# The squares of three group norms: transposed and summed by VectorE, instead of multiplied by a column of ones

## The chip, the cores and the metric

One core of a Trainium2 chip runs the whole program. The time is the device time of one execution in microseconds (us); lower is better. The kernel before takes 617.97 us, the median of three runs (617.78 to 618.43).

Engines, by the names that the profile uses: PE is TensorE's matmul, PEld its weight load, DVE is VectorE, ACT is ScalarE, POOL is GpSimd, SP is SyncE, which issues the DMAs.

## The reference

A two-layer encoder over 256 positions of width 1024, in fp32. Each layer has a mixer of three kinds of attention heads (4 neighbourhood heads "a", 6 dilated heads "d", 6 grouped-query heads "c", each 64 wide) and a channel sublayer (gate, up, a convolution of three taps, gelu, down). What the change touches is the norm of each group's output before the output projection:

```python
def rms_norm(x, g):
    xf = x.astype(jnp.float32)
    y = xf * lax.rsqrt(jnp.mean(xf * xf, axis=-1, keepdims=True) + EPS)
    return (y * g.astype(jnp.float32)).astype(x.dtype)
...
    mix = jnp.concatenate([
        rms_norm(out_a, og[:NA_W]),
        rms_norm(out_d, og[NA_W:NA_W + DIL_W]),
        rms_norm(out_c, og[NA_W + DIL_W:]),
    ], axis=-1)
    return x + mix @ w_out_l
```

So each of the three groups needs, for every one of the 256 positions, the sum of squares over its 256 or 384 columns.

## The kernel before

**Arithmetic.** Large products keep fp32 accuracy by splitting each operand into a high part and a rest (`_hi`/`_lo`, or `act_ch`/`act_cl` for the attention weights): three products stand for one. Weights come by DMA (`wp_raw`); ScalarE casts the high part (`wp_hi`), VectorE subtracts it for the rest (`wp_lo`).

**Layout.** The outputs of the heads stand transposed: 128 features on the partitions, the 256 positions along the free axis, two heads to a tile. When the second head of a pair has been weighed, `mixed` (L1032) makes four things of the pair's PSUM tile: ScalarE writes the high part times the gain (`act_mixT_hi`), VectorE the rest (`act_mixT_lo`), ScalarE the squares (`act_sqm`), and GpSimd adds the squares of the group's pairs up. `group_rstd` (L1047) then has one 128x256 tile of squares and needs the sum over its partitions, with positions on partitions at the end. It is two fp32 products, one for each half of the 256 positions: the squares are the stationary operand, a 128x1 column of ones moves, and each gives one column of a PSUM tile. VectorE copies the two columns out (`small_ss`), and two GpSimd instructions make the factor (`small_ms`, then `small_rstd`). The profile shows each fp32 product as two MATMULs with two weight loads.

**Stages of a layer.** (1) The input projections, as filler between the preparation of queries and keys. (2) Sixteen heads in the order d, c, a: `scores` for a pair of heads (L1126), the softmax (`softens`, L977: maxima on VectorE, two exps and two normalising multiplications for each head on ScalarE, in `act_s2k` tiles), `turn` (L1007: four transposes, then ScalarE's cast `act_ch` and VectorE's rest `act_cl`), `weigh` (L1023: products of `act_ch` and `act_cl` with the values). A `Weave` (L665) puts products of the output projection of the groups that are complete (`out_projections`, L826, tiles `psa_a`) between the heads' work. `group_rstd` is called after the weighing of head 7 (group d), of head 12 (group c) and, for group a, once all heads and the filler are done (L1209). (3) The entrance to the channel sublayer (L1211 to L1267). The last output projections run, first for the left 512 columns, then for the right ones. Each closes with a VectorE instruction that adds the PSUM tile times `small_rstd` to the residual (`const_x`). PE transposes `const_x` in eight 128x128 blocks for each half, ScalarE makes the high part of `act_hT` from them, VectorE the rest. The first block of the gate-and-up products has 16 products with the left half, then needs the right half's transposes. (4) Gate, up and down products, which keep PE busy to the end of the layer.

That makes three group sums a layer and six in all, 12 fp32 products.

**What sets the order.** Nothing is issued as it is written. A `Plan` records every operation, simulates a list schedule with a price for each operation (`cost`, L414), a fixed handover time between engines and a rank that `later(...)` shifts, and emits every engine's stream in the order that this gives. All rows of the profile therefore carry the line of that one emitting statement, L411. The prices that matter here:

```python
        if method == "transpose":
            return 110, 0
        n = args[2].width()
        if args[1].dtype == F32:
            return 108, 0
...
        if method in ("reduce_sum", "reduce_max"):
            n = args[1].width()
```

A VectorE copy or reduction from PSUM is priced at 1.04 ns a column plus 70. Changing one operation's price moves everything that is planned behind it, on all engines.

Of the kernel before, what the change touches and what calls it, by code (L numbers as in the profile page):

```python
# [11 lines left out]
F32 = mybir.dt.float32  # L12
# [4 lines left out]
AX = mybir.AxisListType  # L17

P = 128
S = 256  # L20
NT = S // P
# [198 lines left out]
class Plan:  # L220
# [5 lines left out]
    def pool(self, real, name, bufs, space=bass.MemoryType.SB):  # L226
        return PlanPool(self, real, name, bufs, space)
# [226 lines left out]
def encoder_kernel(  # L454
# [21 lines left out]
    nc = Plan(tc)  # L476
# [3 lines left out]
    const = pool("const", 1)  # L480
# [13 lines left out]
    ident = const.tile([P, P], F32, tag="ident", name="ident")  # L494
# [33 lines left out]
    minus_half = const.tile([P, 32], F32, tag="mh", name="minus_half")  # L528
    nc.gpsimd.memset(minus_half, -0.5)

    ones = const.tile([P, 1], F32, tag="ones", name="ones")
    nc.gpsimd.memset(ones, 1.0)

    vown, vkv = (
        [const.tile([P, NT, 2 * n + 1, HD], F32R, tag=f"v{n}{i}", name=f"v{n}{i}") for i in range(2)]
# [79 lines left out]
    def rstd_of(ss, n, width, eps, name):  # L615

        ms = small.tile([P, n], F32, tag="ms", name=f"ms_{name}")
        nc.gpsimd.tensor_scalar(ms, ss, 1.0 / width, eps, ALU.mult, ALU.add)
        r = small.tile([P, n], F32, tag="rstd", name=f"rstd_{name}")
        nc.gpsimd.tensor_tensor(r, ms, minus_half[:, :n], op=ALU.pow)  # L620
        return r
# [168 lines left out]
    for l in range(DEPTH):  # L790
# [256 lines left out]
        def group_rstd(gi):  # L1047

            _, n = OUTP[gi]
            ps = psw.tile([P, 512], F32, tag="w", name=f"gs{gi}{l}")  # L1050
            for t in range(NT):
                nc.tensor.matmul(
                    ps[:, t : t + 1], hold["sq", gi][:, t * P : (t + 1) * P], ones, start=True, stop=True
                )
            ss = small.tile([P, NT], F32, tag="ss2", name=f"ss_m{gi}{l}")
            nc.vector.tensor_copy(ss, ps[:, :NT])
            group_r[gi] = rstd_of(ss, NT, n * P, EPS, f"m{gi}{l}")
            wv.give(f"mix{gi}")


        hold, turned = {}, {}
# [133 lines left out]
        for i in range(len(heads) + 2):  # L1195
            for part in range(3):
                if (i, part) in hooks:
                    with nc.later(PREP_LATER):
                        hooks[i, part]()
                if part == 0 and i < len(heads) and i % 2 == 0:  # L1200
                    scores(i)
                elif part == 1 and 0 <= i - 1 < len(heads):
                    heads[i - 1].turn()
                elif part == 2 and 0 <= i - 2 < len(heads):
                    weigh(i - 2)
                    if i - 2 in (7, 12):
                        group_rstd((i - 2) // 12)
        wv.fill(1e9)
        group_rstd(2)  # L1209


# [207 lines left out]
```

## Time and profile before

| | us |
|---|---|
| median of three runs (range) | 617.97 (617.78 to 618.43) |
| the profiled execution, device time | 617.81 |
| its span in the profile | 616.0 |
| PE busy | 606.0 |
| DVE busy | 485.8 |
| ACT busy | 428.8 |
| POOL busy | 77.4 |

The device time of the profiled execution is 1.8 us longer than its span; that stretch lies around what the profile covers. The granted clock of TensorE was 0.999 of full speed over the run.

How its rows are read: a row of a timeline has a start, a time in us, the engine, the line, the operation, its output and inputs by the program's names, the tile shapes, and how many neighbouring instructions it groups. A bracket holds the idle time before it and what released it. A matmul's row includes the time until its result is out, so neighbouring rows overlap, and the pace of PE is read from one start to the next.

### The profile page before, as it was taken

What the parts mean: (1) busy time and instruction counts of PE and PEld (TensorE: products, weight loads), DVE (VectorE), ACT (ScalarE), POOL (GpSimd) and SP (SyncE); (2) the same over time, 40 slices, a digit from 0 to 9 for tenths busy, and PEclk for the clock granted to TensorE, in tenths of its full rate; (3) what the DMA queues carried; (4) which work ended last, traced back from release to release, by engine and by line L of the source; (5) the groups of instructions that cost most, each with busy time, mean ns of one, the idle gap of its engine ahead of it and who ended that gap; (6) DMA issues with size and microseconds to landing.
All of it is one profiled execution on the core that took longest, in us unless ns stands there. A gap on an engine that the chain in (4) does not pass through costs nothing.

```text
span 616.0 us, 9844 instructions
## 1 busy us (share of the span) xinstructions
PE 606.0 (98%) x3496; PEld 524.8 (85%) x3496; DVE 485.8 (79%) x1000; ACT 428.8 (70%) x1064; POOL 77.4 (13%) x125
## 2 busy tenths in 40 slices
PE   8999999999999999999999999999999999999997
PEld 6999878888888888888899989887888888888886
DVE  4898988897877877777867798979877777777775
ACT  6888989686566565556588899897756565566551
POOL 2731230211500000000023212112000000000000
PEclk9999999999999999999999999999999999999999
DMA  8894311755596555655444632127575555555501
GB/s 284 274 291 146 103 38 37 245 195 197 183 231 222 178 197 204 199 169 162 155 148 150 233 104 86 34 73 243 182 238 173 191 205 186 169 192 204 168 40 68
DMA packets 81617, 104.66 MB, mean 170 GB/s; under 512 B 9480, under 2 KB 69224, under 8 KB 81568
## 3 DMA queue, kind: packets, MB, share of 16 engines
q1 hardware_dynamic: 81024, 103.78, 52.0%
q8 instruction: 27, 0.44, 0.3%
q10 hardware_dynamic: 544, 0.26, 0.1%
q14 instruction: 22, 0.18, 0.1%
HBM read 102.54 MB, written 1.49 MB: 169 GB/s over the span
## 4 chain that ended last, share of the span: by engine, by line
PE 93%; ACT 3%; DVE 2%; DMA 1%; issue 1%; SPq 0%; ACTq 0%; DVEq 0%
PE psw_w L411 49%; PE psa_a L411 44%; ACT act_s2k L411 2%; DMA wp_raw<-in_w_in_dram 1%; DVE act_hT L411 1%; DVE wp_lo L411 1%; DVE const_x L411 0%; ACT wp_hi L411 0%; ACT act_hT L411 0%; ACT act_ch L411 0%; SPq L411 0%; DVE act_cl L411 0%; DVE act_z L411 0%; ACT const_v L411 0%; DVE small_nm L411 0%
## 5 line engine op out<-in xcount | busy, mean ns | idle before, releaser
L411 DVE TENSOR_TENSOR wp_lo<-wp_raw,wp_hi 128x512 fp32r<-128x512 f32 (+2 forms) x348 | 243.9, 729 | 49.7 <-ACT wp_hi L411 47.8
L411 PE MATMUL psw_w<-act_hT,wp_hi 128*128 128x512 f32 x704 | 247.6, 397 | 2.0 <-DVE act_hT L411 2.0
L411 ACT CAST wp_hi<-wp_raw 128x512 fp32r<-128x512 f32 (+2 forms) x348 | 212.7, 660 | 29.3 <-PE psw_w L411 15.6
L411 PE MATMUL psw_w<-act_hT,wp_lo 128*128 128x256 f32 x704 | 195.7, 279 | 0.0
L411 PEld LDWEIGHTS psw_w<-act_hT,wp_hi 128*128 128x128 f32 x704 | 131.8, 188 | 34.1 <-DVE act_hT L411 3.2
L411 PEld LDWEIGHTS psw_w<-act_hT,wp_lo 128*128 128x128 f32 x704 | 132.6, 188 | 1.2
L411 PE MATMUL psa_a<-wp_hi,act_hT 128*128 128x384 f32 (+2 forms) x448 | 113.1, 333 | 1.3 <-ACT act_hT L411 1.2
L411 ACT COPY act_s2k<-psw_w 128x256 f32<-128x256 f32 x88 | 32.3, 372 | 80.2 <-PE psw_w L411 80.2
L411 PEld LDWEIGHTS psa_a<-wp_hi,act_hT 128*128 128x128 f32 x448 | 77.9, 189 | 4.5 <-ACT act_hT L411 1.6
L411 PE MATMUL psa_a<-wp_lo,act_hT 128*128 128x384 f32 (+2 forms) x224 | 74.6, 334 | 0.0
L411 PE MATMUL psa_a<-wp_lo,act_ch 128*128 128x512 f32 x176 | 69.5, 395 | 0.0
L411 PE MATMUL psa_a<-wp_hi,act_ch 128*128 128x512 f32 x176 | 69.3, 394 | 0.0
L411 PE MATMUL psa_a<-wp_hi,act_cl 128*128 128x512 f32 x176 | 66.1, 394 | 0.0
L411 DVE TENSOR_TENSOR act_s2k<-psw_w,act_s2k 128x256 f32<-128x256 f32 x88 | 36.8, 422 | 32.4 <-ACT act_s2k L411 31.9
L411 PEld LDWEIGHTS psa_a<-wp_lo,act_hT 128*128 128x128 f32 x224 | 42.2, 189 | 1.9 <-DVE wp_lo L411 1.0
L411 PEld LDWEIGHTS psa_a<-wp_hi,act_cl 128*128 128x128 f32 x176 | 33.2, 188 | 7.7
L411 PEld LDWEIGHTS psa_a<-wp_hi,act_ch 128*128 128x128 f32 x176 | 33.1, 188 | 7.8
L411 PEld LDWEIGHTS psa_a<-wp_lo,act_ch 128*128 128x128 f32 x176 | 33.1, 188 | 6.9
L411 DVE SCALAR_TENSOR_TENSOR act_s2k<-act_s2k,act_cw,act_s2k 128x255 f32<-128x255 f32 x88 | 36.7, 476 | 1.4 <-ACT act_s2k L411 1.3
L411 POOL TENSOR_TENSOR small_rstd<-small_ms,const_mh 128x6 f32<-128x6 f32 (+2 forms) x26 | 32.0, 1232 | 2.2
L411 ACT ACTIVATE act_s2k<-act_s2k,act_cw 128x256 f32<-128x256 f32 x44 | 24.1, 595 | 11.6 <-DVE act_s2k L411 11.6
L411 PE MATMUL psw_w<-act_ch,const_v 128*128 128x256 f32 x128 | 28.5, 287 | 1.6 <-ACT act_s2k L411 1.1
(109 smaller groups left out, 754.3 us busy)
## 6 DMA issues: line engine op xcount, KB each, us to landing
wp_raw<-in_w_gate_up_dram SPq DMA_DIRECT2D x44, 1024.0 KB, 5.0
wp_raw<-in_w_down_dram SPq DMA_DIRECT2D x22, 1024.0 KB, 4.8
wp_raw<-in_w_in_dram SPq DMA_DIRECT2D x14, 768.0 KB, 5.9
wp_raw<-in_w_in_dram SPq DMA_DIRECT2D x8, 1024.0 KB, 5.9
wp_raw<-in_w_out_dram SPq DMA_DIRECT2D x8, 768.0 KB, 4.3
wp_raw<-in_w_out_dram SPq DMA_DIRECT2D x4, 512.0 KB, 3.8
act_nab<-dram_scr SPq DMA_DIRECT2D x4, 448.0 KB, 7.0
out_dram<-const_x SPq DMA_DIRECT2D x4, 256.0 KB, 2.0
```

The costliest lines, as they stand in the source:

```text
L411: getattr(o.engine.real, o.method)(*map(real, o.args), **{k: real(v) for k, v in o.kw.items()})
```

## The change

`ones` and its memset go away. In `group_rstd` the two products with the column of ones become two transposes of the squares' halves, which fill 256 columns of the same PSUM tile. The copy of two columns becomes a VectorE sum over the 128 columns of each half. What comes before (the squares and GpSimd's additions) and after (`small_ms`, `small_rstd`) is as it was.

```diff
-    ones = const.tile([P, 1], F32, tag="ones", name="ones")
-    nc.gpsimd.memset(ones, 1.0)
...
             ps = psw.tile([P, 512], F32, tag="w", name=f"gs{gi}{l}")
             for t in range(NT):
-                nc.tensor.matmul(
-                    ps[:, t : t + 1], hold["sq", gi][:, t * P : (t + 1) * P], ones, start=True, stop=True
-                )
+                cols = slice(t * P, (t + 1) * P)
+                nc.tensor.transpose(ps[:, cols], hold["sq", gi][:, cols], ident)
             ss = small.tile([P, NT], F32, tag="ss2", name=f"ss_m{gi}{l}")
-            nc.vector.tensor_copy(ss, ps[:, :NT])
+            nc.vector.reduce_sum(ss, ps[:, :S].rearrange("p (t d) -> p t d", d=P), axis=AX.X)
             group_r[gi] = rstd_of(ss, NT, n * P, EPS, f"m{gi}{l}")
```

The planner now prices each of the two PE operations at 110 instead of 108, and VectorE's at 1.04 x 256 + 70 = 336 instead of 72. From the first group sum of each layer to the entrance of its channel sublayer it gives another order; outside these two stretches (about 90 to 129 us and 390 to 430 us in the profile) the order stays. On SP one pair of DMAs (the convolution's weights of layer 0) is issued one weight load later.

The names in the rows below have buffer numbers, which differ between the programs because one constant is gone. First, PE in layer 0, where the heads of group a are scored for the second time (`act_ko`, `act_qo`: the scores; `act_s2k`: the attention weights to be transposed; `act_ch`, `act_cl` with `const_v`: the weighing). Before:

```order
L411 MATMUL psa_a_157<-wp_lo_252,act_mixT_hi_911 128x512
L411 MATMUL psw_w_123<-const_ident_92,act_s2k_166 128x128
L411 MATMUL psa_a_157<-wp_hi_243,act_mixT_lo_951 128x512
L411 MATMUL psw_w_123<-const_ident_92,act_s2k_166 128x128 x3
L411 MATMUL psw_w_168<-act_ch_858,const_v_107 128x256
L411 MATMUL psw_w_121<-act_ko_567,act_qo_443 128x256
```

Now:

```order
L411 MATMUL psa_a_336<-wp_hi_135,act_mixT_lo_949 128x512
L411 MATMUL psw_w_121<-act_ch_750,const_v_105 128x256
L411 MATMUL psw_w_166<-const_ident_90,act_s2k_164 128x128 x4
L411 MATMUL psw_w_121<-act_cl_768,const_v_105 128x256
L411 MATMUL psw_w_121<-act_ch_750,const_v_110 128x256
L411 MATMUL psw_w_121<-act_ch_750,const_v_105 128x256
L411 MATMUL psw_w_121<-act_cl_768,const_v_105 128x256
L411 MATMUL psw_w_121<-act_ch_750,const_v_110 128x256
L411 MATMUL psw_w_121<-act_ch_856,const_v_105 128x256
```

The first product with the second cast (`act_ch_858` before, `act_ch_856` now) stood right behind the transposes, with the scores behind it; five products of the other head now stand between, and the scores follow after the whole weighing.

Second, ACT in layer 1, at the second sum (group c). `act_s2k` with `small_nm` is an exp, with `small_rs` a normalising multiplication; `act_sqm` are the squares that the second sum waits for; `act_ch` is the cast that the weighing waits for. Before:

```order
L411 ACTIVATE act_mixT_hi_911<-psw_w_168,const_gains_127 128x256
L411 ACTIVATE act_sqm_1006<-psw_w_168 128x256
L411 CAST wp_hi_137<-wp_raw_155 128x512
L411 ACTIVATE act_s2k_177,small_rs_815<-act_s2k_166,small_nm_806 128x256 x2
L411 ACTIVATE act_s2k_131,small_rs_830<-act_s2k_81,small_nm_817 128x256
L411 ACTIVATE act_s2k_177<-act_s2k_177,small_rs_815 128x256 x2
L411 ACTIVATE act_s2k_131,small_rs_830<-act_s2k_81,small_nm_817 128x256
L411 CAST act_ch_858<-psw_w_89 128x512
L411 ACTIVATE act_s2k_131<-act_s2k_131,small_rs_830 128x256 x2
L411 CAST act_ch_752<-psw_w_123 128x512
```

Now:

```order
L411 CAST act_ch_856<-psw_w_87 128x512
L411 ACTIVATE act_mixT_hi_909<-psw_w_121,const_gains_125 128x256
L411 ACTIVATE act_s2k_175,small_rs_813<-act_s2k_164,small_nm_804 128x256 x2
L411 ACTIVATE act_s2k_129,small_rs_828<-act_s2k_81,small_nm_815 128x256 x2
L411 ACTIVATE act_s2k_175<-act_s2k_175,small_rs_813 128x256 x2
L411 ACTIVATE act_s2k_129<-act_s2k_129,small_rs_828 128x256 x2
L411 ACTIVATE act_sqm_1004<-psw_w_121 128x256
L411 CAST act_ch_750<-psw_w_119 128x512
L411 CAST wp_hi_135<-wp_raw_153 128x512 x2
```

The squares stood ahead of all four exps and now stand behind four exps and four multiplications; the cast stood ahead of the last two multiplications and now stands behind all of them and the squares.

Third, PE in layer 1 at the entrance to the channel sublayer. `psa_a` rows are the last output projections, `const_x` rows the transposes of the residual, `act_hT` the first gate-and-up product. Before:

```order
L411 MATMUL psa_a_304<-wp_lo_146,act_mixT_hi_911 128x512
L411 MATMUL psw_w_121<-const_ident_92,const_x_79 128x128
L411 MATMUL psw_w_123<-const_ident_92,const_x_79 128x128
L411 MATMUL psa_a_304<-wp_hi_137,act_mixT_lo_951 128x512
L411 MATMUL psa_a_338<-wp_hi_137,act_mixT_hi_911 128x512
L411 MATMUL psw_w_121<-const_ident_92,const_x_79 128x128 x3
L411 MATMUL psw_w_123<-const_ident_92,const_x_79 128x128 x3
L411 MATMUL psa_a_338<-wp_lo_146,act_mixT_hi_911 128x512
```

Now:

```order
L411 MATMUL psa_a_336<-wp_hi_135,act_mixT_hi_909 128x512
L411 MATMUL psa_a_336<-wp_lo_144,act_mixT_hi_909 128x512
L411 MATMUL psa_a_336<-wp_hi_135,act_mixT_lo_949 128x512
L411 MATMUL psw_w_119<-const_ident_90,const_x_79 128x128
L411 MATMUL psw_w_87<-const_ident_90,const_x_79 128x128
L411 MATMUL psw_w_119<-const_ident_90,const_x_79 128x128 x3
L411 MATMUL psw_w_87<-const_ident_90,const_x_79 128x128 x3
L411 MATMUL psw_w_121<-act_hT_142,wp_hi_241 128x512
```

Before, 20 products of the output projection were left behind the third sum, 13 ahead of the transposes, two among them, five behind. Now 15 are left behind the third sum, and all of them stand ahead of the transposes; five have moved ahead of the sum.

## Prediction

> **What bounds the kernel now.** First the busy times, the granted clock and the chain that ended last, from the page:
>
> ```profile
> PE 606.0 (98%) x3496; PEld 524.8 (85%) x3496; DVE 485.8 (79%) x1000; ACT 428.8 (70%) x1064; POOL 77.4 (13%) x125
> PEclk9999999999999999999999999999999999999999
> PE 93%; ACT 3%; DVE 2%; DMA 1%; issue 1%; SPq 0%; ACTq 0%; DVEq 0%
> ```
>
> PE is busy in 98% of the span and 93% of the chain is PE. So two things change the time: what PE has to do, and the few places where PE stands still. DVE and ACT have room on average, and count where PE waits for them. Those places I looked for in PE's timeline, in the stretches that the new order touches. Layer 0, the heads of group a; the 405.45 row is the same work in layer 1:
>
> ```profile
> 101.86 0.38 PE L411 MATMUL psw_w<-act_ch,const_v 128*128 128x256 f32 x1 [0.34 <-ACT act_ch L411]
> 102.18 1.44 PE L411 MATMUL psw_w<-act_ko,act_qo 64*128 64x256 f32 x12
> 103.55 0.39 PE L411 MATMUL psw_w<-act_cl,const_v 128*128 128x256 f32 x1
> 405.45 0.98 PE L411 MATMUL psw_w<-act_ko,act_qo 64*128 64x256 f32 x12
> 406.36 0.55 PE L411 MATMUL psw_w<-const_ident,act_s2k 128*128 128x128 f32 x3
> ```
>
> PE stands still for 0.34 us until ACT's cast is there. The 12 scores then take 1.37 us to the next start (103.55 - 102.18), where undisturbed ones take 0.91 (406.36 - 405.45): 0.46 more. This place costs 0.8 us. The other two are the entrances to the channel sublayers, with the transposes of the residual and the first products of each half:
>
> ```profile
> 124.11 0.50 PE L411 MATMUL psw_w<-act_hT,wp_hi 128*128 128x512 f32 x1
> 128.74 0.50 PE L411 MATMUL psw_w<-act_hT,wp_hi 128*128 128x512 f32 x1 [0.69 <-DVE act_hT L411]
> ```
>
> ```profile
> 423.84 0.47 PE L411 MATMUL psa_a<-wp_lo,act_mixT_hi 128*128 128x512 f32 x1
> 424.15 0.39 PE L411 MATMUL psa_a<-wp_hi,act_mixT_lo 128*128 128x512 f32 x1
> 424.38 0.40 PE L411 MATMUL psa_a<-wp_hi,act_mixT_hi 128*128 128x512 f32 x1
> 425.20 0.50 PE L411 MATMUL psw_w<-act_hT,wp_hi 128*128 128x512 f32 x1
> 428.11 1.03 PE L411 MATMUL psw_w<-const_ident,const_x 128*128 128x128 f32 x8
> 430.48 0.50 PE L411 MATMUL psw_w<-act_hT,wp_hi 128*128 128x512 f32 x1 [1.34 <-DVE act_hT L411]
> ```
>
> Behind 128.74 and 430.48 PE is kept busy to the end of the layer. I therefore measure the change by how much earlier or later these two products start; what is gained or lost there reaches the end.
>
> **The change part by part. PE's own work.** A pair of products with ones, and transposes of the same kind of tile:
>
> ```profile
> 89.17 0.60 PE L411 MATMUL psw_w<-const_ident,act_s2k 128*128 128x128 f32 x4
> 89.60 0.50 PE L411 MATMUL psw_w<-const_ones,act_sqm 128*128 128x1 f32 x4
> 89.97 0.48 PE L411 MATMUL psa_a<-wp_lo,act_mixT_hi 128*128 128x512 f32 x1
> 121.14 0.38 PE L411 MATMUL psw_w<-const_ident,const_x 128*128 128x128 f32 x2
> 121.27 0.48 PE L411 MATMUL psa_a<-wp_hi,act_mixT_hi 128*128 128x512 f32 x1
> ```
>
> From start to start a pair of products (four rows) takes 89.97 - 89.60 = 0.37 us. Four transposes take 89.60 - 89.17 = 0.43, so two take 0.21; the two of `const_x` take 0.13. I take 0.21, since its input is the same kind of fp32 tile as the squares. The saving is 0.16 a pair (0.24 by the other row), 0.5 us a layer, 1.0 in all.
>
> **VectorE's sum.**
>
> ```profile
> L411 DVE COPY small_ss<-psw_w 128x2 f32<-128x2 f32 x6 | 0.9, 155 | 0.5 <-PE psw_w L411 0.3
> L411 DVE TENSOR_REDUCE small_nm<-psw_w 128x1 f32<-128x256 f32 x24 | 8.7, 416 | 2.5 <-PE psw_w L411 1.8 <-ACT act_s2k L411 0.6
> L411 DVE TENSOR_REDUCE small_ss<-act_s2k 128x8 f32<-128x512 f32 x4 | 2.6, 678 | 0.8 <-ACT act_s2k L411 0.8
> L411 DVE COPY act_rb<-psw_w 128x256 f32<-128x256 f32 x2 | 0.8, 424 | 0.6 <-PE psw_w L411 0.6
> ```
>
> A reduction of 256 columns from PSUM takes 416 ns, the copy 155. One with eight results over 512 columns takes 678, half of it 339. So the sum costs between 0.18 and 0.26 us more than the copy; I take 0.26, from the row with the same columns. [...]
>
> In the groups d and c the sum is behind the heads' work: the products that need its `small_rstd` only close with it, several us later, and DVE is idle 21% of the time. I price these four at nothing; without that cover they would cost 4 x 0.26 = 1.0. The third sum is different: nothing is left to do but the last output projections, which need it.
>
> ```profile
> 419.41 0.27 PE L411 MATMUL psw_w<-const_ident,act_s2k 88*128 88x88 f32 x1
> 420.11 1.03 POOL L411 TENSOR_TENSOR small_rstd<-small_ms,const_mh 128x2 f32<-128x2 f32 x1
> 421.17 1.41 DVE L411 SCALAR_TENSOR_TENSOR const_x<-psa_a,small_rstd,const_x 128x512 f32<-128x512 f32 x2
> ```
>
> The row with 88 columns follows directly behind the third sum on PE and serves as its mark. `small_rstd` is ready 1.73 us after it (421.14 - 419.41), with the new sum 1.99. The two additions to `const_x` take 1.41 more.
>
> **The new order in layer 0.** The scores that stood between two late casts now follow behind the whole weighing, and five more products stand ahead of the second cast's first user. At 0.12 us each (half the 0.23 that 512 columns take at 424.15) these cover 0.6 us, more than the 0.34 of idle time, and the scores no longer stand behind a half-served pair of PSUM tiles. I take the whole 0.8 as saved. With the three pairs (0.5) the third sum's mark comes 1.3 earlier, and less 0.26 for VectorE the first `act_hT` product 1.04 earlier, at 123.07.
>
> Then a loss. Before, seven of the right half's transposes stood among the left half's 16 products; now all eight stand behind them. Sixteen products take 428.11 - 425.20 = 2.91 us in layer 1, where nothing stands among them, and eight transposes 8 x 0.107 = 0.86. From the last transpose to the first product that uses it there are two rows to go by: 1.36 (423.84 to 425.20), and 0.85 from the last one of layer 0:
>
> ```profile
> 126.07 0.93 PE L411 MATMUL psw_w<-const_ident,const_x 128*128 128x128 f32 x7
> 126.75 0.36 PE L411 MATMUL psw_w<-act_hT,wp_lo 128*128 128x256 f32 x1
> ...
> 127.78 0.27 PE L411 MATMUL psw_w<-const_ident,const_x 128*128 128x128 f32 x1
> ```
>
> (127.78 + 0.11 to 128.74.) I take 1.1. So 123.07 + 2.91 + 0.86 + 1.1 = 127.94 against 128.74: layer 0 **gains 0.8**.
>
> **The new order in layer 1.** Here ACT becomes late for the second sum and for the cast that the weighing waits for:
>
> ```profile
> 406.12 0.36 ACT L411 ACTIVATE act_sqm<-psw_w 128x256 f32<-128x256 f32 x1
> 406.93 0.51 ACT L411 ACTIVATE act_s2k<-act_s2k,small_nm 128x256 f32<-128x256 f32 x1
> 408.09 0.51 ACT L411 ACTIVATE act_s2k<-act_s2k,small_nm 128x256 f32<-128x256 f32 x1
> 408.60 0.90 ACT L411 ACTIVATE act_s2k<-act_s2k,small_rs 128x256 f32<-128x256 f32 x2
> 409.40 0.49 ACT L411 ACTIVATE act_s2k<-act_s2k,small_nm 128x256 f32<-128x256 f32 x1
> 409.89 0.56 ACT L411 CAST act_ch<-psw_w 128x512 fp32r<-128x512 f32 x1
> 410.51 0.38 PE L411 MATMUL psw_w<-act_ch,const_v 128*128 128x256 f32 x1 [0.15 <-ACT act_ch L411]
> ```
>
> The first exp starts when its maxima are there, 406.93. Four of them at 0.5 (408.9, or 409.1 if the third starts no earlier than the 408.09 of before), four multiplications at 0.42 (410.8), the squares at 0.36 (411.2), the cast at 0.5 (411.7). Before, this cast was done at 410.45. PE is ready at about 410.7 and waits about 1.1 us where it waited 0.15: **+0.95**. Queued behind it are the second sum, the transposes of the next heads and the fillers behind them; they all move back by as much.
>
> At the entrance five projection products have moved ahead of the third sum: 5 x 0.23 = 1.15. Its mark comes at 419.41 - 0.5 + 0.95 + 1.15 = 421.0. `small_rstd` is ready at 423.0, `const_x` at 424.4; PE has 15 products left, to 421.0 + 15 x 0.23 = 424.5. So both meet, and the transposes start there. Then 0.86 for the eight of them and 1.36: first `act_hT` product at 426.7, against 425.20. With 2.91, 0.86 and 1.1 the second comes at 431.6, against 430.48: layer 1 **loses 1.1**. It is less than at the first because before DVE was late there by its own queue of casts.
>
> **Sum.** -0.8 + 1.1 = +0.3 on the profiled execution's 617.81, so 618.1. The median of the runs shown is 0.16 above that execution: **618.3 us**, no change that a measurement of this kernel can tell (it tells 0.2%, 1.24 us).
>
> **Rivals.**
> 1. **Faster, 616.4.** ACT's lateness in layer 1 is absorbed: the maxima are ready earlier than 406.93, or PE arrives later (-0.95). The pairs take 0.13 (-0.5), and both tails 0.85 instead of 1.1 (-0.5). For it speaks that PE has fewer cycles to spend in any case; against it that four multiplications and the squares really stand ahead of the cast.
> 2. **Slower, 619.6.** In layer 0 PE waits for ACT's cast at another place: the 0.8 is not saved, since the same exps and multiplications have to come before the same casts. The late transposes cost the longer tail, 1.36, in both layers (+0.5). It ends slower once 0.9 of that 1.3 comes about. For it: every new wait found above is on ACT's casts. Against it: the 5 products really are cover.
> 3. **The transposes save nothing on PE**, 619.3: a pair takes the 0.37 of the products, because something other than the number of products sets the pace of this tile (+1.0). Against it the 0.43 for four transposes.
> 4. **The clock falls, 620.5.** Transposes alone are on PE from 424.5 to 426.7. If the clock were halved for as long as they stand without a product, it would cost 2.2 us. Against it this row (sum, then PE, PEld, DVE, ACT and POOL busy, clock, DMA share):
>
> ```profile
> 425.00:432.00 7.00, 5.66 (x34) 4.69 (x33) 7.00 (x15) 6.14 (x15) 2.15 (x3) 1.00 0.72 263
> ```
>
> From 428.11 to 430.48 only transposes ran, for 2.37 us, at a granted clock of 1.00. [...] This trace shows no effect at this length.
>
> **How the numbers follow.** The forecast 0.42, rival 1 0.22, rival 2 0.30, rival 3 0.04, rival 4 0.02. Faster by over 0.2% is rival 1, slower are rivals 2 to 4 together (0.36). The forecast's own range is 616.8 to 619.2. The whole range goes down to 616.2, where layer 1 loses nothing by ACT and the pairs and tails take their lower rows, and up to 620.3, which holds rivals 2 and 3 and the longer tails and uncovered sums in part on top of them.
>
> **What would show it.** Right: pairs of transposes of `act_sqm` at 0.21 from start to start; `small_ss` reductions near 0.42; at 101 to 104 no idle time before `act_ch` products and scores in 0.9; an idle time of about 1 us before an `act_ch` product near 411; `act_hT` second products near 127.9 and 431.6. Wrong: an idle time at other casts of ACT in either layer (rival 2), no idle time near 411 (rival 1), pairs at 0.37 (rival 3), a granted clock under 1 at the entrances (rival 4), or a new stall where the order was not changed.

## The result and the profile after

| | before | changed |
|---|---|---|
| median of 20 executions, us | 618.19 | 619.05 |
| range | 617.57 to 618.68 | 617.80 to 621.36 |
| ratio, 95% interval | | 1.0020 (1.0014 to 1.0026) |
| the profiled execution, device time (span) | 617.81 (616.0) | 620.22 (618.4) |

Slower by 0.86 us in the median: under the 1.24 us that were called a difference, though the interval lies above 1. The spread has grown, and that is the first thing to look at. In 13 of the 20 executions of the changed kernel the mean granted clock was 0.999 or 1.0, and their median is 618.93. In the other seven it was 0.996 or 0.997, and their median is 620.22. The profile is of such an execution. Its page:

```profile
PE 607.4 (98%) x3484; PEld 525.0 (85%) x3484; DVE 488.6 (79%) x1000; ACT 429.0 (69%) x1064; POOL 78.7 (13%) x124
PEclk9999999999999999999999999998999999999999
PE 91%; ACT 4%; DVE 2%; issue 1%; DMA 1%; POOL 1%; SPq 0%; DVEq 0%; ACTq 0%; POOLq 0%
```

One slice of 40 has an 8 where before had a 9. It is layer 1's entrance to the channel sublayer. The windows of the changed kernel (us; PE, PEld, DVE, ACT and POOL busy, clock, DMA share, GB/s), the third of them the row that the prediction showed of before:

```profile
422.91:426.32 3.41, 1.59 (x11) 1.12 (x10) 3.34 (x7) 3.41 (x10) 0.00 (x0) 1.00 0.63 251
426.32:429.74 3.42, 3.42 (x12) 2.94 (x12) 3.42 (x7) 2.38 (x7) 1.85 (x3) 0.50 0.13 33
425.00:432.00 7.00, 5.52 (x24) 4.63 (x24) 5.06 (x11) 4.80 (x14) 1.85 (x3) 0.76 0.41 137
```

PE's timeline of the changed kernel there:

```profile
418.85 0.38 PE L411 MATMUL psw_w<-const_ident,act_sqm 128*128 128x128 f32 x2
419.07 0.24 PE L411 MATMUL psw_w<-const_ident,act_s2k 88*128 88x88 f32 x1
...
422.45 0.40 PE L411 MATMUL psa_a<-wp_hi,act_mixT_lo 128*128 128x512 f32 x1
422.68 0.40 PE L411 MATMUL psw_w<-const_ident,const_x 128*128 128x128 f32 x2
423.30 0.87 PE L411 MATMUL psw_w<-const_ident,const_x 128*128 128x128 f32 x6 [0.22 <-DVE const_x L411]
425.77 0.53 PE L411 MATMUL psw_w<-act_hT,wp_hi 128*128 128x512 f32 x1 [1.60 <-DVE act_hT L411]
...
430.26 1.04 PE L411 MATMUL psw_w<-const_ident,const_x 128*128 128x128 f32 x8
432.30 0.50 PE L411 MATMUL psw_w<-act_hT,wp_hi 128*128 128x512 f32 x1 [1.01 <-DVE act_hT L411]
```

From the last output projection to the first `act_hT` product there are 3.32 us with eight transposes only (422.45 to 425.77). Half a microsecond after PE is at work again, its clock goes to a half for 3.42 us. The 16 products take 4.49 us (425.77 to 430.26) where they took 2.91: 1.58 lost.

Layer 0 is earlier, as forecast. The same three places of the changed kernel as in the prediction's first fences, the scores, the first and the second `act_hT` product:

```profile
101.39 0.60 PE L411 MATMUL psw_w<-const_ident,act_s2k 128*128 128x128 f32 x4
...
103.28 0.98 PE L411 MATMUL psw_w<-act_ko,act_qo 64*128 64x256 f32 x12
104.19 0.50 PE L411 MATMUL psa_a<-wp_hi,act_mixT_hi 128*128 128x512 f32 x1
...
122.86 0.50 PE L411 MATMUL psw_w<-act_hT,wp_hi 128*128 128x512 f32 x1
127.81 0.50 PE L411 MATMUL psw_w<-act_hT,wp_hi 128*128 128x512 f32 x1 [1.01 <-DVE act_hT L411]
```

The scores take 0.91 and nothing waits for ACT's cast; the second product starts at 127.81 instead of 128.74. So the profile is 0.93 ahead at layer 0's entrance and 1.82 late at layer 1's (432.30 against 430.48), of which 1.58 is the clock. Of the 0.93, 0.11 is there ahead of all that changed, as one VectorE row of before and the same row of the changed kernel show:

```profile
86.14 0.41 DVE L411 TENSOR_TENSOR act_z<-act_z,act_gna 128x256 f32<-128x256 f32 x1
86.02 0.41 DVE L411 TENSOR_TENSOR act_z<-act_z,act_gna 128x256 f32<-128x256 f32 x1
```

The last product starts 2.38 later than before (614.36 against 611.98), so another 0.56 comes behind 432.30, where the order did not change. More of such jumps are told of below, with the table by layer.

### The profile page after: what moved, and what is told of

It reads as the page before. It is cut to its first block, busy times and chain, and to the rows that moved or that the text cites. A ratio compares the mean times of both kernels' runs of the same rounds, so it can differ in the third digit from the quotient of the medians.

```text
span 618.4 us, 9823 instructions
## 1 busy us (share of the span) xinstructions
PE 607.4 (98%) x3484; PEld 525.0 (85%) x3484; DVE 488.6 (79%) x1000; ACT 429.0 (69%) x1064; POOL 78.7 (13%) x124
## 4 chain that ended last, share of the span: by engine, by line
PE 91%; ACT 4%; DVE 2%; issue 1%; DMA 1%; POOL 1%; SPq 0%; DVEq 0%; ACTq 0%; POOLq 0%
PE psw_w L411 49%; PE psa_a L411 42%; ACT act_s2k L411 2%; DVE const_x L411 1%; DMA wp_raw<-in_w_in_dram 1%; ACT act_hT L411 1%; ACT wp_hi L411 1%; DVE act_hT L411 0%; POOL small_rstd L411 0%; SPq L411 0%; DVE wp_lo L411 0%; ACT act_ch L411 0%; DVE act_mixT_lo L411 0%; POOL small_ms L411 0%; ACT act_mixT_hi L411 0%
```

## The experiments

Everything behind a changed price moves, so instructions and order had to be parted. A field of the planner sets the price of single operations; with it the changed instructions can be planned at the old prices and the other way about:

```diff
-        o.ns, o.size = cost(engine.name, method, args, kw, ins)
+        o.ns, o.size = cost(engine.name, method, args, kw, ins); o.ns = self.price or o.ns
...
+                nc.price = 108
                 nc.tensor.transpose(ps[:, cols], hold["sq", gi][:, cols], ident)
+            nc.price = 72.08
             ss = small.tile([P, NT], F32, tag="ss2", name=f"ss_m{gi}{l}")
             nc.vector.reduce_sum(ss, ps[:, :S].rearrange("p (t d) -> p t d", d=P), axis=AX.X)
+            nc.price = None
```

Two theories go through the expectations. By theory 1 the new order makes the difference, by theory 2 VectorE's longer sum does. In gaps and products_in_gap, theory 1 is what the expectation there says of the clock.

With the old prices every engine's rows stand as before, but for the sums themselves. This is **old_order**:

> The changed instructions in the order of before (the planner is told the prices of before, 108 and 72 ns, for the transposes and the sum of the squares). Theory 1, the order makes the difference: PE saves about 0.2 us at each of six sums and the third sum of each layer costs 0.26 more, so 617.2 to 617.8 where before has 618.2; no stretch near 425 us without plain products longer than before's 2.4 us, granted clock 1.00 there in all profiles. Theory 2, VectorE's longer sum makes the difference: 618.9 or more, the loss at the third sum of each layer.

618.64 against 617.97, ratio 1.0006 (0.9997 to 1.0015), clock full in all 11 executions. (The medians alone give 1.0011; the ratio lies nearer to that of the means.) Neither theory as it stood: the saving that the first expected isn't there, and nothing shows that it is slower either.

**new_order_ones** keeps the products with ones and sets `nc.price = 110` for them and 336.24 for the copy, which gives the changed kernel's order:

> The products with ones kept, in the order of the change (the planner is told 110 and 336 ns for them). Theory 1: slower than before although no instruction is changed, 619.5 to 621.5, about 1 us over the changed kernel's runs with the clock at 1.00 (618.9) and with a granted clock of about 0.5 for 3.4 us near 426 us in part of the executions. Theory 2: 618.2, as before.

618.84 against 617.97, ratio 1.0015 (1.0006 to 1.0024): the order alone costs 0.9 us with no instruction changed. The time is below the 619.5 to 621.5 that were expected, and the clock did not fall in any of the 11 executions, which was not expected either.

**new_order_layer0** is old_order with the old prices in layer 1 only (`nc.price = 108 if l == 1 else None`, likewise the sum):

> The changed instructions; the new order in layer 0 only, layer 1 in the order of before. Theory 1: the lead of 1.4 us that the changed kernel's profile has at the start of layer 1 is kept and layer 1 loses nothing: 616.3 to 617.0, clock 1.00 at layer 1's entrance. Theory 2: as the changed kernel's runs at full clock, 618.9.

617.40, ratio 0.9993 (0.9984 to 1.0002), full clock in all 11: on the right side, but 0.4 over the range.

**new_order_layer1** has them in layer 0 only:

> The changed instructions; the new order in layer 1 only, layer 0 in the order of before. Theory 1: the loss of layer 1's entrance without layer 0's lead: 619.3 to 620.0 at full clock, 1.5 more in executions with the clock at about half near 426 us, whose share may differ from the changed kernel's 7 in 20. Theory 2: 618.9.

619.72 in five executions, ratio 1.0038 (1.0024 to 1.0052). Three at full clock have 619.62; in two the clock fell (620.77 and 621.72). So the new order gains in layer 0, loses in layer 1, and the fall of the clock belongs to layer 1.

**changed_again** is the changed kernel once more:

> The changed kernel once more. If the clock's fall near 426 us comes by chance from one execution to the next, about a third of the executions show a mean clock of 0.996 to 0.997 and 619.9 to 621.4, the others 617.8 to 619.4. If it belonged to the chip of the first run, none or all do here.

618.71 against 617.87, ratio 1.0019 (1.0009 to 1.0028). Two of 11 executions were at 0.996 and 0.997 (620.07 and 620.62), the others from 617.58 to 619.23: by chance from one execution to the next.

**products_in_gap** puts eight products that nobody uses between the transposes and the first `act_hT` product of layer 1, at a price that leaves all else in its place:

```diff
+        if l == 1:
+            nc.price = 1
+            for i in range(8):
+                nc.tensor.matmul(cps[:, 256:512], h2_hi[:, 0, :P], h2_hi[:, 0], start=True, stop=True)
+            nc.price = None
         _, r2 = mean_squares(f"n2{l}")
```

> The changed kernel with eight more products of 256 columns at layer 1's entrance, between the transposes and the first act_hT product; their result is not used. They start when ScalarE's first act_hT block is there, so the stretch without plain products shrinks from 3.3 to about 2.4 us and ends no later. Theory 1, a stretch of over about 3 us without plain products lets the clock fall: no execution under 0.998, all at 617.8 to 619.5, median 618.9. Rival, the clock falls for another reason (the moment, the load): a third of the executions at 619.9 to 621.4 as before.

No execution of ten under 0.999; the median is 618.67, as that of the changed kernel's full-clock executions (618.49), with one at 620.10 at 0.999. With a third of the executions, none in ten would come up in 2 of 100 cases (0.67 to the tenth), so this speaks for theory 1 without settling it.

**gaps** settles it, by one profiled execution with many gaps. Behind the last layer it runs blocks of 24 products with gaps between them, in which PE has to wait for a chain on ScalarE:

```diff
+    def block(g, kind, m):
+        ps = psw.tile([P, 512], F32, tag="w", name="gp")
+        for _ in range(24):
+            nc.tensor.matmul(ps, g[:, :P], g, start=True, stop=True)
+        if kind != "idle":
+            p2 = psw.tile([P, 512], F32, tag="w", name="gq")
+            for _ in range(4 + 2 * m):
+                if kind == "turn":
+                    nc.tensor.transpose(p2[:, :P], ident, ident)
+                else:
+                    nc.tensor.matmul(p2[:, :S], g[:, :P], g[:, :S], start=True, stop=True)
+        z = act.tile([P, 512], F32, tag="s2k", name="gz", bufs=NS2K)
+        scaled(z, ps, 0.01)
+        for _ in range(m):
+            scaled(z[:, :P], z[:, :P], 1.0)
...
+GAPS = [("idle", m) for m in (2, 4, 6, 8, 10, 12)] * 2
+GAPS += [("turn", m) for m in (6, 8, 10, 12)] * 2 + [("product", m) for m in (8, 12)] + [("idle", 3)]
```

> The changed kernel with a measurement behind its last layer (the result is the same; the time is longer by the measurement): blocks of 24 plain products, between them gaps that ScalarE's chain makes, of about 2 to 5 us, either empty, or filled with transposes, or filled with plain products. Theory 1: empty gaps under 2.8 us leave the granted clock at 1.00, those well over 3.3 us let it fall to about 0.5 for some 3.4 us; gaps filled with transposes do the same as empty ones of that length; gaps filled with plain products leave it at 1.00. Rival: transposes count as work, so filled gaps stay at 1.00 and in the changed kernel only the idle 1.6 us would have mattered, too short to let an empty gap fall.

Pairs of windows of this kernel, each a gap and the products behind it (columns as above). First an empty gap and one with 28 transposes, equally long:

```profile
672.48:678.30 5.82, 0.38 (x2) 0.00 (x0) 0.00 (x0) 4.93 (x14) 0.00 (x0) 0.85 0.00 0
678.30:686.01 7.71, 7.71 (x24) 6.21 (x24) 0.00 (x0) 0.00 (x0) 0.00 (x0) 0.67 0.00 0
785.04:790.88 5.84, 3.45 (x31) 3.12 (x29) 0.00 (x0) 4.94 (x14) 0.00 (x0) 1.00 0.00 0
790.88:796.23 5.35, 5.35 (x24) 4.42 (x24) 0.00 (x0) 0.00 (x0) 0.00 (x0) 1.00 0.00 0
```

The empty gap costs the clock (0.67 over the products behind it), the one with transposes doesn't (1.00). So theory 1 is wrong in its second half: **transposes counted as work**. All ten empty gaps of 3.1 us and over were followed by a fall; of eight with transposes, 3.8 to 5.8 us long, one was. (The two gaps meant for plain products were longer than their products: 2.0 and 2.4 us stayed empty, and a fall followed on the second.) Now two empty gaps of the same length:

```profile
618.20:620.62 2.42, 0.39 (x3) 0.00 (x1) 0.00 (x0) 1.84 (x4) 0.00 (x0) 1.00 0.00 0
620.62:627.59 6.97, 6.97 (x24) 5.59 (x24) 0.00 (x0) 0.00 (x0) 0.00 (x0) 0.76 0.01 2
686.01:688.42 2.41, 0.39 (x2) 0.00 (x0) 0.00 (x0) 1.84 (x4) 0.00 (x0) 1.00 0.00 0
688.42:693.78 5.36, 5.36 (x24) 4.43 (x24) 0.00 (x0) 0.00 (x0) 0.00 (x0) 1.00 0.01 3
```

So the rival was right that transposes count, and wrong that a short idle time can't cost the clock (0.76 behind 2.42 us). But one gap is followed by a fall and the other isn't, so length alone does not decide. What does is in the moments at which the clock changed, from this profile's records:

```
falls from 1.0 to 0.5 at 621.95 632.19 642.43 652.67 662.91 676.56 697.04 707.28 717.52 731.18 744.83 768.72 854.06 us
each lasting 3.41 or 6.83 us
```

Their distances are 10.24, 13.65, 20.48 us and so on: 3, 4 and 6 times 3.413. So I read the records as windows of 3.413 us, one behind the other, with the clock changing at their ends. Such windows, by how long PE was busy in them:

```profile
618.54:621.95 3.41, 1.38 (x7) 1.11 (x7) 0.00 (x0) 1.84 (x4) 0.00 (x0) 1.00 0.02 5
628.78:632.19 3.41, 1.50 (x6) 1.24 (x7) 0.00 (x0) 1.73 (x5) 0.00 (x0) 1.00 0.00 0
686.80:690.21 3.41, 1.78 (x8) 1.48 (x9) 0.00 (x0) 1.48 (x4) 0.00 (x0) 1.00 0.02 5
765.31:768.72 3.41, 1.51 (x9) 1.08 (x8) 0.00 (x0) 2.04 (x6) 0.00 (x0) 1.00 0.00 0
806.27:809.68 3.41, 1.68 (x16) 1.43 (x14) 0.00 (x0) 3.12 (x10) 0.00 (x0) 1.00 0.00 0
```

Behind 1.38, 1.50 and 1.51 us of busy time the clock fell; behind 1.68 (transposes alone) and 1.78 it stayed. The changed kernel's window 422.91 to 426.32, with 1.59, is of those that fall: in these records the bound lies between 1.59 and 1.68 of 3.41 us. In every profile the clock also changes near the end, so there too the windows can be laid back from that moment. In the changed kernel's profile it falls again at 617.47, 56 windows behind 426.32. In changed_again it falls at 615.18, 55 windows behind 427.44; the window at the entrance that ends there has 1.82 us, and no fall follows:

```profile
424.03:427.44 3.41, 1.82 (x12) 1.41 (x10) 3.34 (x8) 3.41 (x12) 0.00 (x0) 1.00 0.42 171
```

Laid so over all 13 profiles, every window at full clock with up to 1.59 us is followed by a fall and none with 1.68 or more.

This explains the chance. The windows lie differently against the work from one execution to the next: one ends 0.55 us behind the first `act_hT` product in the changed kernel's profile (425.77 to 426.32), 1.37 behind it in changed_again's (426.07 to 427.44). In the changed kernel's profile a window of 3.41 us has 1.59 to 1.66 us of busy time wherever it starts between 422.3 and 423.1, and more elsewhere: 0.8 to 0.9 us of 3.41 possible positions, a quarter, if each is as likely as the next. The clock fell in 11 of the 36 executions with this entrance (7 of 20, 2 of 11, 2 of 5), which fits a quarter. In products_in_gap no position has under 2.48 us. It explains new_order_ones too. The stretch is 2.83 us there, and no position of the window has less than this:

```profile
422.60:426.01 3.41, 1.85 (x13) 1.43 (x12) 3.17 (x6) 3.41 (x11) 0.00 (x0) 1.00 0.87 334
```

Part of what makes the stretch half a microsecond longer with transposes (3.32 against 2.83) is the third sum, and it is also what was missing in old_order. GpSimd and VectorE in layer 0, before and in old_order, the same order:

```profile
118.85 0.19 POOL L411 TENSOR_SCALAR small_ms<-small_ss 128x2 f32<-128x2 f32 x1 [1.11 <-DVE small_ss L411]
118.61 0.15 DVE L411 COPY small_ss<-psw_w 128x2 f32<-128x2 f32 x1
118.74 0.25 DVE L411 COPY act_cw<-psw_w 128x88 f32<-128x88 f32 x1
118.91 0.68 DVE L411 TENSOR_TENSOR wp_lo<-wp_raw,wp_hi 128x512 fp32r<-128x512 f32 x1
```

```profile
119.46 0.72 POOL L411 TENSOR_SCALAR small_ms<-small_ss 128x2 f32<-128x2 f32 x1 [1.37 <-DVE small_ss L411]
120.26 0.71 POOL L411 TENSOR_TENSOR small_rstd<-small_ms,const_mh 128x2 f32<-128x2 f32 x1
118.95 0.42 DVE L411 TENSOR_REDUCE small_ss<-psw_w 128x2 f32<-128x256 f32 x1
119.28 0.24 DVE L411 COPY act_cw<-psw_w 128x88 f32<-128x88 f32 x1
119.44 0.68 DVE L411 TENSOR_TENSOR wp_lo<-wp_raw,wp_hi 128x512 fp32r<-128x512 f32 x1
```

GpSimd's `small_ms` took 0.19 us before (118.85, just ahead of VectorE's `wp_lo` at 118.91). Behind the longer sum it comes at the moment at which `wp_lo` begins (119.46 and 119.44), and takes 0.72: it ends with it (120.18 and 120.12). The rows show the two durations, not what makes the one longer; that it is `wp_lo` is my reading of them. From the third pair's start on PE, `small_rstd` is ready after 2.09 us in both layers of before; in old_order it takes 2.57 in layer 0 (118.40 to 120.97) and 2.87 in layer 1.

The changed kernel has the same in layer 0 (`small_ms` 0.72, 2.57 from the pair's start). At layer 1's entrance its `small_ms` keeps 0.19, and the instruction behind it is the one that meets `wp_lo`. First the changed kernel, then new_order_ones, in the same order with products:

```profile
420.59 1.21 POOL L411 TENSOR_TENSOR small_rstd<-small_ms,const_mh 128x2 f32<-128x2 f32 x1
420.54 0.69 DVE L411 TENSOR_TENSOR wp_lo<-wp_raw,wp_hi 128x512 fp32r<-128x512 f32 x1 [0.17 <-ACT wp_hi L411]
```

```profile
420.70 0.71 POOL L411 TENSOR_TENSOR small_rstd<-small_ms,const_mh 128x2 f32<-128x2 f32 x1
421.15 0.69 DVE L411 TENSOR_TENSOR wp_lo<-wp_raw,wp_hi 128x512 fp32r<-128x512 f32 x1 [0.65 <-ACT wp_hi L411]
```

`small_rstd` is ready 2.95 us behind the third pair's start (418.85 to 421.80) with transposes and 2.18 with products (419.23 to 421.41). Of these 0.77 only 0.29 arrives at the first `act_hT` product (6.92 against 6.63 from the pair's start). The rest of the half microsecond, 0.19, is PE's own saving: its pair is shorter (0.22 against 0.41), so it runs out of products that much earlier.

If that is so, group a alone should keep its products with ones. **ones_for_a** does that, in the order of new_order_layer0:

```diff
+                nc.price = 110 if l == 0 else 108
+                if gi == 2:
+                    nc.tensor.matmul(ps[:, t : t + 1], hold["sq", gi][:, cols], ones, start=True, stop=True)
+                else:
+                    nc.tensor.transpose(ps[:, cols], hold["sq", gi][:, cols], ident)
+            nc.price = 336.24 if l == 0 else 72.08
...
+            if gi == 2:
+                nc.vector.tensor_copy(ss, ps[:, :NT])
+            else:
+                nc.vector.reduce_sum(ss, ps[:, :S].rearrange("p (t d) -> p t d", d=P), axis=AX.X)
```

> Transposes for the groups d and c, products with ones for group a alone (the third sum), in the order of new_order_layer0. If the third sum's longer way through VectorE is what eats the saved PE time, 0.3 to 0.5 us a layer come back and two pairs' saving of 0.15 each is lost: 616.7 to 617.2, against 617.4. If the third sum costs nothing more, 617.7.

616.59 against 617.87, ratio 0.9978 (0.9969 to 0.9987), clock full in all 11: faster than both kernels, and 0.1 better than the range. In its profile `small_ms` is back at 0.19 us:

```profile
418.38 0.16 DVE L411 COPY small_ss<-psw_w 128x2 f32<-128x2 f32 x1
...
418.63 0.19 POOL L411 TENSOR_SCALAR small_ms<-small_ss 128x2 f32<-128x2 f32 x1 [1.11 <-DVE small_ss L411]
418.91 1.02 POOL L411 TENSOR_TENSOR small_rstd<-small_ms,const_mh 128x2 f32<-128x2 f32 x1
```

Three more kernels fill the table of instructions and orders. **ones_for_a_old_order** (108 and 72.08 throughout):

> Transposes for the groups d and c, products with ones for group a, everything in the order of before. If four pairs save 0.15 to 0.2 us each and VectorE's sums of d and c are hidden, 617.1 to 617.4 where before has 617.9. If old_order's lost saving had another cause than the third sum, it stays at 618.3 to 618.6.

617.37 against 617.87, ratio 0.9994 (0.9985 to 1.0003): within the range of the first reading, though the interval holds 1. **ones_for_a_new_order** (110 and 336.24 throughout):

> The same instructions in the order of the changed kernel in both layers. The stretch without plain products at layer 1's entrance is 2.8 us again as in new_order_ones, so no execution has a clock under 0.998; with the third sum's price gone, 0.7 below the changed kernel's full-clock runs: 617.7 to 618.3. If the fall of the clock is tied to the new order and not to the length of the stretch, a third of the executions lies 1.5 us higher.

618.52, ratio 1.0007 (0.9998 to 1.0016), full clock in all 11. The fall goes with the stretch (2.82 us here) and not with the order; the median is 0.2 above the range. **ones_new_order_layer0** is new_order_ones with the new prices in layer 0 only:

> No transposes of squares at all: the products with ones of before, with the new order in layer 0 alone. If the new order of layer 0 is worth its 1 us by itself, 616.9 to 617.2, and the four transposed pairs of ones_for_a (616.6) are worth the other 0.3 to 0.6. If the transposes made the whole gain, 617.9 as before.

617.18, ratio 0.9987 (0.9978 to 0.9996). The order of layer 0 brings 0.7 by itself.

Differences to the median of before taken beside each run, us. Executions in which the clock fell are left out. An interval is about 0.5 to either side, 0.9 for the five executions of new_order_layer1, so two cells have to differ by some 0.7 before it means anything.

| order | products with ones | transposes for d and c, ones for a | transposes for all |
|---|---|---|---|
| of before | 0 | -0.50 | +0.67 |
| new in layer 0 | -0.69 | -1.28 | -0.57 |
| new in layer 1 | not run | not run | +1.65 |
| new in both | +0.87 | +0.65 | +0.74, again +0.62 |

The profiles tell it more closely, if they are compared from mark to mark. The marks are VectorE's last `act_z` instruction ahead of each changed stretch (86.14 and 386.95 in before) and the second `act_hT` product behind it (128.74 and 430.48). How much longer the way from one to the other takes than in before, us, one number for each profile, at full clock:

| stretch and order | products with ones | transposes for d and c, ones for a | transposes for all |
|---|---|---|---|
| layer 0, of before | 0 | -0.42 | -0.02, +0.01 |
| layer 0, new | -0.66, -0.71 | -1.13, -1.14 | -0.77 to -0.81 (five) |
| layer 1, of before | 0, +0.04 | -0.05, 0.00 | +0.42, +0.47 |
| layer 1, new | +1.58 | +1.32 | +1.62, +1.63, +1.63 |

(The profile of the changed kernel shown above has +3.23 in layer 1, with 1.58 of the clock in it; products_in_gap has +1.71, with its extra products.) Profiles of one cell agree within 0.05. Read down, the new order brings 0.7 to 0.8 in layer 0 and costs 1.2 to 1.6 in layer 1. Read across, the two pairs for d and c save 0.4 to 0.5 in layer 0; in layer 1 they save nothing in the old order and 0.3 in the new. The third sum by transposes costs 0.3 to 0.5 in each layer, also in the new order, where the medians of the last row do not show it; there it brings the falls besides.

Starts on the profile's clock can't be compared so closely. At 86 us, ahead of every edit, the profiles lie from 0.66 ahead of before's to 0.75 behind it. In 4 of the 12 other profiles layer 1 begins 0.5 earlier behind layer 0's entrance than in before, and in 6 of 11 the last product comes 0.55 later behind layer 1's entrance, without an edit there. The cause of these jumps stays open.

## Why the prediction held, and where it did not

- **The time**: forecast 618.3, at 617.97 for before, so +0.33, in a range of 616.2 to 620.3. Measured 619.05, +0.86. The sign of the sum is right, the size is not: +0.7 at full clock, and 1.3 us more (620.22 less 618.93) in some three executions of ten. By layer, from mark to mark and at full clock: forecast -0.8 and +1.1, measured -0.8 and +1.6.
- **The pair on PE**: taken as 0.21, with 0.13 as its lower end. Measured from start to start 0.14 to 0.22 where nothing is waited for (418.85 to 419.07). The duration is right. What the pairs are worth is not: 0.5 a layer was counted for three of them, and the two for d and c brought 0.4 to 0.5 in layer 0 and 0 to 0.3 in layer 1, while the third was outweighed by its longer sum.
- **VectorE's sum**: taken as 0.42. Measured by group of the changed kernel:

```profile
L411 DVE TENSOR_REDUCE small_ss<-psw_w 128x2 f32<-128x256 f32 x6 | 2.5, 416 | 0.1
```

  Right, and those of d and c are hidden in layer 0, where their pairs gain 0.42 in the old order. In layer 1 the same pairs gain nothing in the old order, and why stays open. But "with the new sum 1.99" behind the third sum's mark, which is 2.20 from the pair's start (1.99 and the 0.21 of the pair), was too little: it measured 2.57 and 2.87 in the old order, 2.57 and 2.95 in the changed kernel, because a GpSimd instruction that starts together with `wp_lo` on VectorE took 0.5 longer (0.72 against 0.19, 1.21 against 0.71). Only the sum's own duration was counted, not what comes to stand beside it.
- **Layer 0's order**: forecast a gain of 0.8, 127.94 for the second `act_hT` product; measured 127.81, a gain of 0.93, of which 0.11 was there at 86 us already. So 0.82, as forecast. The scores take 0.91 again and the eight late transposes cost what was reckoned. The gain is the order's, as ones_new_order_layer0 shows; the 0.5 counted for PE's pairs is partly taken back by the third sum.
- **ACT's lateness in layer 1**: forecast 0.95. The profile has an idle time of 0.60 at that product:

```profile
405.67 0.51 ACT L411 ACTIVATE act_s2k<-act_s2k,small_nm 128x256 f32<-128x256 f32 x1
...
409.52 0.57 ACT L411 CAST act_ch<-psw_w 128x512 fp32r<-128x512 f32 x1
```

```profile
410.14 0.39 PE L411 MATMUL psw_w<-act_ch,const_v 128*128 128x256 f32 x1 [0.60 <-ACT act_ch L411]
```

  The rank of events was right, its price 0.45 instead of 0.95. That the exps begin at 405.67 and not at 406.93 is not the reason, since PE comes earlier too: the wait is 0.60 to 0.61 also in new_order_layer1, new_order_ones, changed_again and ones_for_a_new_order, which begin layer 1 from 0.55 to 1.81 us ahead of before. From the first exp to the end of the cast ACT took 4.42 us (405.67 to 410.09), where 4.77 was forecast (406.93 to 411.7). And PE was free 3.87 us behind the first exp (410.14 less 0.60), where 3.77 was forecast.
- **Layer 1's entrance**: forecast a loss of 1.1, measured 1.62 to 1.63 at full clock, clear of the 0.05 within which profiles agree. Two terms were off and in opposite directions. ACT's lateness cost 0.5 less. But from the row with 88 columns to the first `act_hT` product it took 6.70 us (419.07 to 425.77) where 5.7 was forecast (421.0 to 426.7): `small_rstd` was ready 2.73 behind that row and not 1.99, PE waited once more for `const_x` among the transposes, and from the first transpose to the product there were 3.09 us (422.68 to 425.77) and not 2.2. The way from the first to the second product was right: 4.95 in changed_again (426.07 to 431.02), forecast 4.9. That the first product stands near the forecast 426.7 less layer 0's lead of 0.8 is luck: this profile begins layer 1 with a lead of 1.41, and changed_again with 1.09.
- **The rival that the clock falls** had a chance of 0.02. It happened in 11 of 36 executions. The failed step is the comparison "from 428.11 to 430.48 only transposes ran, for 2.37 us, at a granted clock of 1.00": it compared lengths of stretches, and its own stretch was forecast too short (2.2 us from the first transpose, where it was 3.09). In the records the fall goes with PE's busy time within windows of 3.41 us: before had 2.07 us at the worst position, the changed kernel 1.59; both the stretch's length and the window's position decide. Nor does a run show the clock halved for as long as the transposes stand alone, from which the rival's 2.2 us came: it was 1.00 up to 426.32 and 0.50 behind that, for 3.42 us, which cost 1.58.
- **The slower rival** (ACT's casts in layer 0, long tails) did not happen: layer 0's saving is there. **The faster one** came out half in ACT's lateness and not in the tails.

The kernel that would have been worth making is ones_for_a: 616.59, with transposes where their sum is hidden and the products where it is waited for. Not tried: a third sum by transposes with VectorE's `wp_lo` moved away from behind it.

## What to carry to other kernels

Price a longer instruction by what it comes to stand beside, not by its duration alone: 0.26 us of VectorE became 0.5 to 0.8 at GpSimd's result. Where a scheduler sets the order from prices, run the new instructions with the old prices and the old instructions with the new ones; the two differences here (+0.67 and +0.87 in the medians, +0.4 and +0.9 over both layers of the profiles) would have been read as one. Compare profiles from a mark ahead of the edit to one behind it: their starts differ by up to 0.75 us before any edit. And a stretch in which PE mostly waits had a second price here, 1.58 us behind a window with 1.59 us of busy time in 3.41, so look at the busy time in such windows before making one longer.

## What the runs showed of the hardware

- In gaps the granted clock went to a half for 3.41 or 6.83 us, at moments whose distances are multiples of 3.413 us. From full clock it fell behind windows in which PE was busy for up to 1.51 us (1.59 in the changed kernel), and stayed behind those with 1.68 and more. From half clock, 2.67 us of busy time (731.18 to 734.59 in gaps) did not bring it back and 3.08 (707.28 to 710.70) did.
- Transposes counted as busy time: in gaps, a gap of 5.84 us with 28 of them kept the clock at 1.00, an empty one of 5.82 lost it (0.67 over the products behind it).
- GpSimd's `small_ms` took 0.72 us where it started 0.02 from the start of VectorE's `wp_lo` (119.46 in old_order, 117.60 in the changed kernel), and 0.19 where it started 0.06 ahead of it (118.85 in before). `small_rstd` took 1.21 where it started 0.05 behind that of `wp_lo` (420.59 in the changed kernel), and 0.71 where `wp_lo` came 0.45 later (420.70 in new_order_ones).
